# A hybrid layer on one core: the start of the first token block, the stores of its p results, and the last spread of 1/rms

## The chip, the cores and the metric

The kernel runs on one core of a Trainium2 chip. The metric is the time of one execution on the device, in microseconds (us). The engines are named as the profile names them: PE is the matrix engine (PEld its weight loads), DVE the vector engine, ACT the scalar engine, POOL the general engine, SP the engine that only issues transfers. Each engine works through its own queue of instructions in order; a transfer (DMA) is issued by an instruction on SP, ACT or POOL and then runs by itself.

## The reference

One encoder layer over 2048 prompt tokens and, with a state of their own, 64 sample tokens. All is float32, the model width is 1024.

```python
h = rms_norm(x, g_pre)
vA, bA, cA, zA, q, f, iv, zB, gA, gB = split_cols(h @ w_in)          # 10 projections of 1024
yA = (silu(zA) * bA * causal_conv3(cA * vA, conv_w)) @ w_a_out       # path A
S_new, o = hgrn2_scan(S0, silu(q) * scale, 1 - fg, iv, log(fg))      # path B, chunks of 64, 8 heads
   # fg = lb + (1 - lb) * sigmoid(f);  lb from a softmax over lb_raw, the "lower bounds"
yB = (rms(o) * g_onorm * silu(zB)) @ w_b_out
out = (sigmoid(gA) * yA + sigmoid(gB) * yB) @ w_o
x = x + rms_norm(out, g_post)
x = x + (p @ w_ple_proj) * sigmoid(rms_norm(x, g_ple) @ w_ple_gate)  # p: 256 columns per token
```

The outputs are x for both kinds of tokens, the last two rows of the convolution's input and the states S.

## The kernel before

The 2112 tokens are cut into three blocks of 768, 704 and 640. Within a block everything lies with features on the 128 partitions and tokens along the free axis; a block has two token halves (`segs`), and a product covers 128 x 128 weights and one half of 384, 352 or 320 tokens. Each float32 number is split into a rounded high part and a low remainder (`split`: the high part is a copy on ACT, the low part a subtraction on DVE), and each product is three: high x high, high x low, low x high. Many products of the large projections use a Strassen-like scheme of seven products for eight (`sgroup`, `in_turn`).

Tiles come from rings: `rt` gives one of 48 tiles of full block width, `hf` one of 8 of half width, `ps_attn` one of 3 banks for results of products and `ps_gemm` one of 5 others. A Python program writes the instructions; a scheduler orders them per engine by priority and expected readiness. Code under `tc.high_priority()` goes first. `placed()` puts instructions behind the last product so far, `behind_all(marks)` behind the named instructions, and `paced(dma)` makes a transfer wait for the last product so far. `hook()` takes the next entry of a list, so that side work is put between groups of products.

The start (in `hybrid_step`, from line 1417) has these steps:

- ACT issues the loads `vec` (the gain vectors and lb_raw) and `hist_s`. SP issues, in this order, two tiles of p of block 0 (`load_p`, `ph0`), four tiles of `w_ple`, eight tiles of rows of x (`ask_rows`), two of `w_ple`, four of rows, two of `w_ple`, p of block 1, one tile of x by features (`ask_x`), four halves of weights (`ask_w`) and seven tiles of x.
- `split_p` splits p; `held_split(j)` splits tile j of `w_ple`, which is kept for two blocks. The generator `ple` then makes p @ w_ple_proj: each of its eight steps j is 12 products (two halves, two tiles of p, three products each), and its result is copied out of the bank (L1212 on DVE, L1214 on ACT) and stored to memory by POOL (L1219).
- Between the first steps of `first_ple` stand the squares of the rows of x (L1484 on ACT, L1481 and L1482 on DVE), whose mean gives 1/rms; `rstd_of` raises to the power -0.5 on POOL (L682), and `spread` (L693) lays the result over all partitions with products against the identity.
- `first_operands` scales x (L787) and makes its high and low parts and the sums for the seven-product scheme. Meanwhile `plain_group` multiplies the last two column groups of gB as x comes, one feature tile k at a time; before each k `next_k` runs a step of `second_ple` (the same `ple` for block 1) and one step of `first_operands`.
- `constants` makes masks, clears tiles and computes the lower bounds `lb` (L207 to L216).

The end: in the last block `norms` are the final norms of the two token halves and `gate` the last products (w_ple_gate) of each half. `spread_out` gives each hook a number of steps of a norm. In `rms`, one step sums squares over partitions (`col_rstd`, L702) and starts the power on POOL, and the next spreads the result (`spread`, L693, copied by L713). Then eight steps make the operands of the second half's products (L1365 and the split). `final_gate` puts off its merges (L1374, L1375) by a table `held`, from group j to a number of merges; those of the last entry stand behind the copy of the spread, those of earlier ones behind the mean.

Of the kernel before, what the change touches and what calls it, by code (L numbers as in the profile page):

```python
# [18 lines left out]
P = 128  # L19
# [74 lines left out]
def hybrid_step(  # L94
# [73 lines left out]
        return dram.tile([P, BN], F32, tag=f"{kind}{j}", name=nm(kind), bufs=2)[:, : width[0]]  # L168


    ident = const.tile([P, P], F32, tag="ident", name="ident")
    make_identity(nc, ident)
    ones = const.tile([P, 1], F32, tag="ones", name="ones")
# [21 lines left out]
    def constants():  # L195
        for rows, odd, base in ((slice(0, P), 0, 0), (slice(0, CH), 1, -CH), (slice(CH, P), 1, CH)):
            tri = rt(P)
            G.memset(tri, 1.0)
            G.affine_select(
                out=tri, in_=tri, pattern=[[1, P]], compare_op=ALU.is_ge, fill=0.0, base=base, channel_multiplier=-1  # L200
            )
            V.tensor_copy(caus[odd][rows], tri[rows])
        V.memset(keep, 1.0)
        V.memset(keep.rearrange("p (c t) -> p c t", t=CH)[:, :, 0:1], 0.0)
        for t in atts + lone:
            V.memset(t, 0.0)
        V.tensor_tensor(tmp, lb0, lb1, ALU.max)  # L207
        V.tensor_tensor(lb, lb0, tmp, ALU.subtract)
        V.tensor_tensor(omlb, lb1, tmp, ALU.subtract)
        A.activation(lb, lb, AF.Exp)  # L210
        A.activation(omlb, omlb, AF.Exp)
        V.tensor_tensor(tmp, lb, omlb, ALU.add)
        V.reciprocal(tmp, tmp)
        V.tensor_tensor(lb, lb, tmp, ALU.mult)
        V.tensor_scalar(omlb, lb, -1.0, 1.0, ALU.mult, ALU.add)
        V.tensor_scalar(nomlb, lb, 1.0, -1.0, ALU.mult, ALU.add)  # L216
# [269 lines left out]
    def plain_group(i1, i2, hs, sink, raws=None, between=None):  # L486


        w, ps = {}, {}

        def split_of(c, h):
            key = ((i1, i2)[c], h)
            raw = raws[c, h] if raws else load_raw(w_blk[key])
            with nullcontext() if raws else tc.high_priority():
                w[c, h] = split_w(raw, key)

        for c, h in ((0, 0), (1, 0)) if between else ((0, 0), (0, 1), (1, 0), (1, 1)):
            with behind_all(() if between else summed[2] if c else ends[-1]):
                split_of(c, h)

        def add(c, ks):
            for k in ks:
                hi, lo = w[c, k // KH]
                for h in range(2):
                    if (c, h) not in ps:
                        ps[c, h] = ps_gemm()
                    xhi, xlo = hs[k][h]
                    T.matmul(ps[c, h], hi[:, k % KH, :], xhi, start=k == 0, stop=False)
                    T.matmul(ps[c, h], hi[:, k % KH, :], xlo, start=False, stop=False)
                    last[0] = T.matmul(ps[c, h], lo[:, k % KH, :], xhi, start=False, stop=k == KB - 1).ins  # L510

        if between:
            for k in range(KB):
                between()
                for c in range(2):
                    if k == 2:
                        split_of(c, 1)
                    with placed():
                        add(c, (k,))
        for c in range(2):  # L520
            if not between:
                with placed():
                    add(c, range(KB))
            for h in range(2):
                sink(c, h, ps[c, h], None)
# [652 lines left out]
            hooks.extend([None, None, None, piece] * 12)  # L1178


    def load_p(bl, queue):
        raws = [rt(), rt()]
        for k, raw in enumerate(raws):
            queue.dma_start(raw, p_fm[k * P : (k + 1) * P, bl["t0"] : bl["t0"] + bl["n"]])
        return raws

    def ple(bl, ph, kept, held=None, shared=False, spare=()):
# [3 lines left out]
        for j in range(KB):  # L1191
# [23 lines left out]
            if bl["last"]:  # L1215
                kept["p", j] = t
            else:
                kept["p", j] = spill("p", j)
                G.dma_start(kept["p", j], t)  # L1219
                if not shared:  # L1220
                    lows["p", j] = dram.tile([P, 2, P], F32, tag=f"lop{j}", name=nm("low"), bufs=1)
                    SP.dma_start(lows["p", j], lo.bitcast(F32))
# [193 lines left out]

    kepts = [{} for _ in blocks]
    width[0] = blocks[0]["n"]
    A.dma_start(vec, vecs)
    A.dma_start(hist_s, hist0)  # L1420

    with tc.high_priority():
        ph0 = load_p(blocks[0], SP)
        raws = [rt(4 * P).rearrange("p (j k c) -> p j k c", j=2, c=P) for _ in range(KH)]
        raws = [raw[:, j] for raw in raws for j in range(2)]
        rows, xs, w1 = [], [], {}
# [2 lines left out]
        def ask_ple(*js):  # L1429
            for j in js:  # L1430
                SP.dma_start(raws[j], w_ple[j])

        def ask_rows(n):
            for r, c in places[len(rows) : len(rows) + n]:
# [9 lines left out]
            for c in range(2):  # L1444
                w1[c, h] = load_raw(w_blk[GB * 8 + KB - 2 + c, h])

        ask_ple(0, 1, 2, 3)
        ask_rows(8)
        ask_ple(4, 5)
        ask_rows(4)  # L1450
# [2 lines left out]
            ph1 = load_p(blocks[1], SP)  # L1453
        ask_x(1)
        ask_w(0)
        ask_w(1)
        ask_x(7)
        held = []

        def held_split(j):  # L1460
# [6 lines left out]
            out = [(rt(dt=F32R), rt(dt=F32R)) for _ in raws]  # L1467
            return out, [split(raw, *hl) for raw, hl in zip(raws, out)][-1]

        ph, done = split_p(ph0)  # L1470
        with behind_all(done):
            done = [held_split(j) for j in range(2)][-1]
    first_ple = ple(blocks[0], ph, kepts[0], held, True)

    ss = small.tile([P, 2, 6], F32, tag="rows", name="rows", bufs=1)
    for n in range(4):
        with behind_all((*done, *evicted)):
            for i in range(3 * n, 3 * n + 3):
                t, total = rows[i], ss[:, i % 2, i // 2 : i // 2 + 1]
                if i % 3 == 2:  # L1480
                    V.tensor_tensor(t, t, t, ALU.mult)  # L1481
                    V.tensor_reduce(total, t, axis=mybir.AxisListType.X, op=ALU.add)  # L1482
                else:
                    A.activation(t, t, AF.Square, accum_out=total)  # L1484
            if n == 3:
                V.tensor_tensor(ss[:, 0, :], ss[:, 0, :], ss[:, 1, :], ALU.add)
                done = [*done, rstd_of(ss[:, 0, :], ss[:, 0, :], 1.0 / D)]
        with placed():
            run(first_ple, 1)
        with behind_all(done):  # L1490
            for j in (n + 2,) if n < 3 else (5, 6, 7):
                done = held_split(j)
    for _ in range(2):
        with placed():
            run(first_ple, 1)
# [11 lines left out]
    ops = first_operands(hc, rs, xs, hs)  # L1507
    second_ple = sized(blocks[1], ple(blocks[1], ph, kepts[1], held, spare=(1, 3, 5)))

    with behind_all(done):  # L1510
        run(ops, 2)

    def next_k():

        with placed():
            run(second_ple, 2 if len(hs) == 2 else 1)
        if len(hs) < KB:
# [5 lines left out]
        plain_group(GB * 8 + KB - 2, GB * 8 + KB - 1, hs, gate_sink(outs, opened), w1, next_k)  # L1523
    keep_gates(kepts[0], GB, KB - 2, outs)
    run(second_ple)
    with behind_all((*copies, *opened)):
        run(ops)
    constants()
    fills = sized(blocks[0], gates(blocks[0], hc, kepts[0], True))
    for bi, bl in enumerate(blocks):  # L1530
        first, kept = bi == 0, kepts[bi]
# [83 lines left out]
            run(final_gate(bl, segs, xo, h2, kept))  # L1615
        else:

            gate = [final_gate(bl, [s], xo, h2, kept, anew=s is segs[1], held={} if s is segs[1] else {0: 0, 1: 0, 2: 0, 3: 2, 4: 3}) for s in segs]
            spread_out((norms[0], (2, 2, 1, 0, 1, 1, 4, 4)), (norms[1], (0,) * 6 + (1, 1) + (1, 1, 1, 0, 0, 1, 1, 3, 3, 2)))
            run(ple(bl, ph, kept, spare=range(KB)))  # L1620
            run(gate[0], 2)
            with behind_all(copies[:1]):
# [53 lines left out]
```

## Time and profile before

| | us |
|---|---|
| median of three runs (lowest, highest) | 2593.07 (2592.7, 2595.34) |
| the profiled execution | 2591.23 |
| its span, first to last instruction | 2589.5 |
| PE busy in that span | 2567.9 |
| DVE, ACT and POOL busy | 1726.6, 1530.7, 367.5 |

The profile shows one execution on the chip. A page gives sums; views of the trace give the instructions in order of time (start, duration, engine, line, output and inputs, and in brackets the idle time before it and what ended it), the waits (who waited for whom: total, times, longest), groups of instructions by line (count, busy time, mean ns, idle time before them), stretches of time with the busy time of each engine, the granted clock of PE as a share of full speed, and the transfers. `PEq`, `SPq` and the like are the sequencers of the engines, which issue transfers. Durations of products overlap: the step from one start to the next is what counts.

### The profile page before, as it was taken

What the parts mean: (1) busy time and instruction counts of PE and PEld (TensorE: products, weight loads), DVE (VectorE), ACT (ScalarE), POOL (GpSimd) and SP (SyncE); (2) the same over time, 40 slices, a digit from 0 to 9 for tenths busy, and PEclk for the clock granted to TensorE, in tenths of its full rate; (3) what the DMA queues carried; (4) which work ended last, traced back from release to release, by engine and by line L of the source; (5) the groups of instructions that cost most, each with busy time, mean ns of one, the idle gap of its engine ahead of it and who ended that gap; (6) DMA issues with size and microseconds to landing.
All of it is one profiled execution on the core that took longest, in us unless ns stands there. A gap on an engine that the chain in (4) does not pass through costs nothing.

```text
span 2589.5 us, 47473 instructions
## 1 busy us (share of the span) xinstructions
PE 2567.9 (99%) x16414; PEld 2554.4 (99%) x16414; DVE 1726.6 (67%) x3495; ACT 1530.7 (59%) x2973; POOL 367.5 (14%) x675
## 2 busy tenths in 40 slices
PE   8999999999999999999999999999999999999999
PEld 8999999999999999999999999999999999999998
DVE  7788778898767775466464556987345545346967
ACT  6766676454453764466564555576456655446675
POOL 2011111230022021111111221102100000001011
PEclk9999999999999999999999999999999999999999
DMA  8678777898797888877778999989887788999985
GB/s 325 218 262 287 270 255 273 309 375 305 260 347 244 272 313 265 282 251 232 260 225 291 344 388 313 326 290 335 292 270 249 247 271 268 297 299 323 331 267 197
DMA packets 361457, 739.87 MB, mean 286 GB/s; under 512 B 44374, under 2 KB 49024, under 8 KB 361216
## 3 DMA queue, kind: packets, MB, share of 16 engines
q1 hardware_dynamic: 321696, 582.69, 67.5%
q0 software_dynamic: 39232, 154.10, 16.3%
q8 instruction: 129, 2.11, 0.3%
q14 instruction: 112, 0.92, 0.1%
q10 hardware_dynamic: 288, 0.05, 0.0%
HBM read 543.44 MB, written 193.22 MB: 284 GB/s over the span
## 4 chain that ended last, share of the span: by engine, by line
PE 91%; DMA 3%; DVE 3%; issue 2%; ACT 1%; POOL 0%; SPq 0%; DVEq 0%; ACTq 0%; POOLq 0%
PE pg L436 19%; PE pg L438 19%; PE pg L437 19%; PE pg L587 5%; PE pg L586 5%; PE pg L588 5%; PE pg L626 3%; PE pg L624 3%; PE pg L625 3%; PE pa L1129 1%; PE pa L1089 1%; PE pa L1131 1%; PE pa L1075 1%; DMA s<-low 1%; PE pa L1074 1%
## 5 line engine op out<-in xcount | busy, mean ns | idle before, releaser
L436 PE MATMUL pg<-r,hi 128*128 128x320 f32 (+2 forms) x3304 | 1086.0, 329 | 1.5 <-DVE r L484 0.9
L437 PE MATMUL pg<-r,hi 128*128 128x320 f32 (+2 forms) x3304 | 1066.6, 323 | 0.0
L438 PE MATMUL pg<-r,lo 128*128 128x384 f32 (+2 forms) x2356 | 767.8, 326 | 2.6 <-DMA lo<-low 2.6
L267 ACT CAST hi<-raw 128x512 fp32r<-128x512 f32 x730 | 449.7, 620 | 518.8 <-PE pg L437 175.1
L436 PEld LDWEIGHTS pg<-r,hi 128*128 128x128 f32 x3304 | 621.3, 188 | 3.1 <-issue 1.5
L437 PEld LDWEIGHTS pg<-r,hi 128*128 128x128 f32 x3304 | 621.6, 188 | 0.0
L438 PEld LDWEIGHTS pg<-r,lo 128*128 128x128 f32 x2356 | 442.3, 188 | 3.7 <-DMA lo<-low 3.6
L438 PE MATMUL pg<-r,s 128*128 128x352 f32 (+1 forms) x948 | 300.0, 316 | 1.2 <-DMA s<-low 1.1
L587 PE MATMUL pg<-r,hi 128*128 128x320 f32 (+2 forms) x864 | 277.2, 322 | 0.5 <-DVE r L220 0.4
L586 PE MATMUL pg<-r,hi 128*128 128x320 f32 (+2 forms) x864 | 274.9, 322 | 0.0
L220 ACT CAST hi<-raw 128x512 fp32r<-128x512 f32 x252 | 155.5, 620 | 156.0 <-PE pg L625 40.1
L220 DVE TENSOR_TENSOR r<-r,r 128x320 fp32r<-128x320 f32 (+7 forms) x352 | 208.5, 611 | 52.3 <-ACT r L220 51.1
L220 DVE TENSOR_TENSOR lo<-raw,hi 128x512 fp32r<-128x512 f32 x231 | 158.3, 687 | 87.7 <-ACT hi L220 83.9
L220 ACT CAST r<-r 128x320 fp32r<-128x320 f32 (+7 forms) x352 | 185.4, 559 | 50.5 <-DMA r<-w_blk 12.9
L588 PE MATMUL pg<-r,lo 128*128 128x352 f32 (+2 forms) x564 | 180.9, 321 | 1.1 <-DMA lo<-low 1.1
L438 PEld LDWEIGHTS pg<-r,s 128*128 128x128 f32 x948 | 178.1, 188 | 2.1 <-DMA s<-low 2.1
L624 PE MATMUL pg<-r,hi 128*128 128x384 f32 (+2 forms) x512 | 167.3, 328 | 0.2 <-ACT hi L267 0.2
L625 PE MATMUL pg<-r,hi 128*128 128x384 f32 (+2 forms) x512 | 167.3, 327 | 0.0
L220 ACT CAST hi<-s 128x512 fp32r<-128x512 f32 x156 | 96.1, 618 | 120.3 <-PE pg L437 107.0
L587 PEld LDWEIGHTS pg<-r,hi 128*128 128x128 f32 x864 | 162.2, 188 | 2.1 <-DVE r L220 1.6
L586 PEld LDWEIGHTS pg<-r,hi 128*128 128x128 f32 x864 | 161.3, 188 | 1.3 <-ACT r L220 0.9
L450 ACT COPY hf<-pg 128x352 f32<-128x352 f32 (+2 forms) x354 | 157.1, 446 | 1.9 <-PE pg L438 1.6
(398 smaller groups left out, 4113.3 us busy)
## 6 DMA issues: line engine op xcount, KB each, us to landing
raw<-w_blk SPq DMA_DIRECT2D x577, 256.0 KB, 4.1
raw<-S SPq DMA_DIRECT2D x444, 256.0 KB, 4.1
lo<-low SPq DMA_DIRECT2D x422, 256.0 KB, 4.0
s<-low SPq DMA_DIRECT2D x308, 256.0 KB, 4.0
low<-lo SPq DMA_DIRECT2D x271, 256.0 KB, 3.7
S<-s SPq DMA_DIRECT2D x152, 256.0 KB, 3.5
low<-r POOLq DMA_DIRECT2D x54, 256.0 KB, 4.9
r<-w_blk POOLq DMA_DIRECT2D x52, 256.0 KB, 6.8
```

The lines of the kernel that those rows point to most:

```text
L220: return A.copy(hi, src).ins, V.tensor_tensor(lo, src, hi.bitcast(F32), ALU.subtract).ins
L267: A.copy(hi, raw)
L436: add(hi[:, k, :], xhi, start=start and k == 0, stop=False)
L437: add(hi[:, k, :], xlo, start=False, stop=False)
L438: last[0] = add(lo[:, k, :], xhi, start=False, stop=k == KH - 1).ins
L450: copied = A.copy(got[n], ps[bank])
L586: add(hi[:, k, :], xhi, start=start and k == 0, stop=False)
L587: add(hi[:, k, :], xlo, start=False, stop=False)
L588: last[0] = add(lo[:, k, :], xhi, start=False, stop=k == KH - 1).ins
L624: T.matmul(ps, hi[:, k % 4, :], xhi[:, c], start=k == ks[0], stop=False)
L625: T.matmul(ps, hi[:, k % 4, :], xlo[:, c], start=False, stop=False)
L626: last[0] = T.matmul(ps, lo[:, k % 4, :], xhi[:, c], start=False, stop=k == ks[-1]).ins
```

## The change

- Eleven products of a cleared 128 x 128 tile with itself stand first in PE's queue; their result is not read.
- p of block 0 is loaded in four parts, by token halves, with the first tile of `w_ple` behind the first part; the splits follow in the same halves, with the first tile of `w_ple` split after the first part and the second after the fourth. The order of later loads changes too: two tiles of x come between the two pairs of weights.
- The loads `vec` and `hist_s` stand behind these splits, and the lower bounds are a function of their own, placed behind all splits of `w_ple`.
- The results of `ple` for blocks 0 and 1 are not stored at once: `store_parked` stores them from the fourth tile of x on, two or three before each k, each waiting for the last product so far.
- One step of `second_ple` is put ahead of the first operands, and the second half of the first weights is split behind the third tile's operands.
- At the end, the spread of the second half's last 1/rms moves from the hook in group 4 to the hook in group 5, the steps behind it are taken as 4 and 4, and the merges held for it are released after group 5 (four of them) and not after group 4 (three).

```diff
+    idle = hf(P)
+    V.memset(idle, 0.0)
+    unread = ps_attn()
+    for _ in range(11):
+        T.matmul(unread[:, :P], idle, idle, start=True, stop=True)
     ident = const.tile([P, P], F32, tag="ident", name="ident")
...
         for t in atts + lone:
             V.memset(t, 0.0)
+
+    def lower_bounds():
         V.tensor_tensor(tmp, lb0, lb1, ALU.max)
...
                     if k == 2:
-                        split_of(c, 1)
+                        with behind_all(ends[2]):
+                            split_of(c, 1)
...
+    parked = []
+
+    def store_parked(n):
+
+        for _ in range(min(n, len(parked))):
+            paced(G.dma_start(*parked.pop(0)))
...
-                G.dma_start(kept["p", j], t)
+                if held is not None:
+                    parked.append((kept["p", j], t))
+                else:
+                    G.dma_start(kept["p", j], t)
...
-    A.dma_start(vec, vecs)
-    A.dma_start(hist_s, hist0)
 
     with tc.high_priority():
-        ph0 = load_p(blocks[0], SP)
+        ph0 = [rt(), rt()]
...
+        def ask_p(h):
+            for k, raw in enumerate(ph0):
+                SP.dma_start(half(raw, h), p_fm[k * P : (k + 1) * P, h * hn() : (h + 1) * hn()])
+                if k == 0 and h == 0:
+                    ask_ple(0)
...
-        ask_ple(0, 1, 2, 3)
+        assert blocks[0]["t0"] == 0
+        ask_p(0)
+        ask_p(1)
+        ask_ple(1, 2, 3)
         ask_rows(8)
...
         ask_x(1)
         ask_w(0)
+        ask_x(2)
         ask_w(1)
-        ask_x(7)
+        ask_x(5)
...
-        ph, done = split_p(ph0)
+        ph, done = [(rt(dt=F32R), rt(dt=F32R)) for _ in ph0], ()
+        for h in range(2):
+            for k, (raw, (hi, lo)) in enumerate(zip(ph0, ph)):
+                with behind_all(done):
+                    done = split(half(raw, h), half(hi, h), half(lo, h))
+                if k == h:
+                    with behind_all(done):
+                        done = held_split(h)
         with behind_all(done):
-            done = [held_split(j) for j in range(2)][-1]
+            A.dma_start(vec, vecs)
+            A.dma_start(hist_s, hist0)
...
+    split_all = done
...
-    with behind_all(done):
+    with placed():
+        run(second_ple, 1)
+    with behind_all((*done, *copies)):
         run(ops, 2)
 
     def next_k():
 
+        store_parked((0, 0, 0, 2, 2, 3, 3, 3, 3)[len(hs)])
         with placed():
             run(second_ple, 2 if len(hs) == 2 else 1)
...
     run(second_ple)
+    store_parked(len(parked))
     with behind_all((*copies, *opened)):
         run(ops)
     constants()
+    with behind_all(split_all):
+        lower_bounds()
...
-            gate = [final_gate(bl, [s], xo, h2, kept, anew=s is segs[1], held={} if s is segs[1] else {0: 0, 1: 0, 2: 0, 3: 2, 4: 3}) for s in segs]
-            spread_out((norms[0], (2, 2, 1, 0, 1, 1, 4, 4)), (norms[1], (0,) * 6 + (1, 1) + (1, 1, 1, 0, 0, 1, 1, 3, 3, 2)))
+            gate = [final_gate(bl, [s], xo, h2, kept, anew=s is segs[1], held={} if s is segs[1] else {0: 0, 1: 0, 2: 0, 3: 2, 4: 0, 5: 4}) for s in segs]
+            spread_out((norms[0], (2, 2, 1, 0, 1, 1, 4, 4)), (norms[1], (0,) * 6 + (1, 1) + (1, 1, 1, 0, 0, 1, 0, 1, 4, 4)))
```

## The prediction

> **What bounds the kernel now.** I read the page first, then the waits of the matrix engine, the chain of waits over the first 100 us, the order of time there, and the same at the end.
>
> ```profile
> span 2589.5 us, 47473 instructions
> PE 2567.9 (99%) x16414; PEld 2554.4 (99%) x16414; DVE 1726.6 (67%) x3495; ACT 1530.7 (59%) x2973; POOL 367.5 (14%) x675
> ```
>
> PE is busy for all but 21.6 us. So this change can gain only idle time of PE, or time in which PE runs at a lower clock. The waits of PE over the whole run name both places that the diff touches:
>
> ```profile
> PE pa L1207 <- ACT r L220: 6.8, 1, 6.8
> PE pa L693 <- POOL cols L682: 1.1, 2, 0.8
> ```
>
> The first is the start. The chain there, and the rows in order of time:
>
> ```profile
> 0.81 3.45 DMA vec<-vecs
> ...
> 5.46 0.18 DVE lbt L214
> ```
>
> ```profile
> 0.81 0.86 SPq L1184 DMA_DIRECT2D r<-p_fm  x2
> 0.88 0.06 DVE L174 MEMSET ones<- 128x1 f32 x1 [0.88 <-PEq L1664]
> ...
> 2.78 0.45 DVE L206 MEMSET lone<- 128x128 f32 x3
> ...
> 4.90 2.16 ACT L220 CAST r<-r 128x768 fp32r<-128x768 f32 x4
> ...
> 6.80 0.69 PE L1207 MATMUL pa<-r,r 128*128 128x384 f32 x1 [6.80 <-ACT r L220]
> ...
> 8.51 0.52 PE L1207 MATMUL pa<-r,r 128*128 128x384 f32 x1
> ...
> 12.35 0.37 PE L1207 MATMUL pa<-r,r 128*128 128x384 f32 x1
> ...
> 26.54 1.50 PE L693 MATMUL pa<-ident,rows 128*128 128x128 f32 x12
> ```
>
> PE idles 6.80 us: the lower bounds (lbt) stand on the path ahead of the splits of p. Then it steps by 0.32 us a product (12 from 8.51 to 12.35), and by 0.175 after that (the other 81 of the first `ple`'s 96, to 26.54): 5.55 us at half the clock. At 26.54 the spread of 1/rms (L693) begins. At the end of the kernel:
>
> ```profile
> 2537.42 0.31 PE L624 MATMUL pg<-r,hi 128*128 128x320 f32 x1
> ...
> 2541.95 0.31 PE L625 MATMUL pg<-r,hi 128*128 128x320 f32 x1
> 2542.40 0.83 PE L702 MATMUL pa<-ones,r 128*128 128x1 f32 x6
> ...
> 2543.47 0.31 PE L625 MATMUL pg<-r,hi 128*128 128x320 f32 x1
> 2544.62 1.24 PE L693 MATMUL pa<-ident,cols 128*128 128x128 f32 x6 [0.84 <-POOL cols L682]
> ```
>
> ```profile
> 2545.05:2548.45 3.40, 3.40 (x16) 3.40 (x15) 2.55 (x7) 0.62 (x1) 1.59 (x4) 0.51 0.33 118
> 2541.62:2545.03 3.41, 2.43 (x17) 1.90 (x16) 2.38 (x7) 1.10 (x3) 1.15 (x2) 1.00 0.99 368
> ...
> 2516.90:2525.00 8.10, 7.87 (x57) 7.55 (x58) 3.54 (x9) 5.06 (x13) 4.27 (x7) 1.00 0.75 237
> ```
>
> The columns of the last fence are the stretch, its length, the busy times of PE, weight loads, DVE, ACT and POOL, the clock, the DMA share and GB/s. PE steps every 0.146 us (31 from 2537.42 to 2541.95), so it could go on at about 2543.62 and goes on at 2544.62: 1.0 us lost to the power of -1/2 on POOL. A stretch of 3.41 us with PE busy 2.43 us is followed by 3.40 us at a granted clock of 0.51. That is 3.40 x 0.49 = 1.67 us more.
>
> **Weighed against the skill.** The Trainium skill, "TensorE: Matmul & The Clock Gate", Part 1, says the gate watches free-running windows of 3413 ns, releases the clock after one busy window and halves it after one idle window. The width agrees with the 3.40 us row; the condition does not, since the window ahead of it was 2.43 us busy. By the page's rule of a whole idle window the end could gain only the 1.0 us, and the sum below would be smaller by 1.67 us. I go by the row.
>
> **The change, part by part.**
>
> *Products of zeros.* They wait for one memset. DVE's first row is at 0.88 and a 128x128 memset is 0.45 / 3 = 0.15 us, so PE starts at about 1.1. Eleven products in f32 are 22 instructions (three columns of L693 give six). The L693 row at half clock is 1.24 us for six, 0.207 each: 4.55 us, to 5.65. They add that to PE in a stretch where it was idle to 6.80, so they cost nothing unless the real operands are there before 5.65; that loss is at most about 1 us.
>
> *Clock.* Before, the clock rose 5.55 us after the first product. From 1.1 that gives 6.65; counted in windows of 3.4 us with unknown phase it is 4.5 to 7.9. At worst PE makes real products at half speed from 5.65 to 7.9, 1.1 us lost.
>
> *p by halves, lower bounds behind the splits, small loads behind them.* The first product needs half of one p tile, one w_ple tile and their splits, not two whole p tiles and nine small lbt operations. Four loads take the place of two on SP, and at about 0.43 us an issue (0.86 for two) the loads queued behind them, rows of x first, are asked for up to 0.9 us later; but they no longer share the queue with `vecs`. I count these as equal. The first split can then start near 3.5 to 4, and PE starts real work at 5.65, set by the products of zeros.
>
> *What is late next.* 96 products x 0.174 = 16.7 us from 5.65 would end at 22.35: the lower bound. Before, cold PE hid ACT; now ACT sets the pace. It carries squares, splits of w_ple and copies in order:
>
> ```profile
> L1484 ACT ACTIVATE r<-r 128x512 f32<-128x512 f32 x8 | 5.0, 628 | 1.7 <-DMA r<-x_tok 1.7
> L220 ACT CAST r<-r 128x256 fp32r<-128x256 f32 x6 | 2.4, 409 | 0.2 <-DMA r<-w_ple 0.2
> L1214 ACT COPY r<-pa 128x384 f32<-128x384 f32 x4 | 1.9, 476 | 1.1 <-PE pa L1209 0.9
> ```
>
> ```profile
> 1.73 1.28 ACT L210 ACT_TABLE_LOAD   x1 [1.73 <-PEq L1664]
> 8.42 0.63 ACT L1484 ACTIVATE r<-r 128x512 f32<-128x512 f32 x1 [1.36 <-DMA r<-x_tok]
> 18.56 0.41 ACT L220 CAST r<-r 128x256 fp32r<-128x256 f32 x1 [0.16 <-DMA r<-w_ple]
> ```
>
> From 8.42 to 18.97 are 10.55 us, about 9.0 of them work (idle: 1.7 less the 1.36 ahead of 8.42, 0.2 and 1.1). The table load may now stand in front of the first square and the two issues of small loads (0.9 us, as two on SP) after the splits, which end near 6.0: 6.0 + 0.9 + 1.28 = 8.2, about as early as the row of x came before. Then 8.2 + 9.0 = 17.2 for the last split of w_ple, the sixth some 0.7 earlier, and with its DVE half and waits PE starts the sixth of eight steps at about 17.3 and ends at 17.3 + 3 x 2.09 = 23.6. The upper end is 26.54, no gain. I take 23.6, nearest to ACT's own row: **2.9 us gained** (bounds 0 and 4.2).
>
> *Stores of p behind the loads of x.* POOL's sixteen stores leave this stretch:
>
> ```profile
> p<-r POOLq DMA_DIRECT2D x8, 384.0 KB, 6.5
> p<-r POOLq DMA_DIRECT2D x8, 352.0 KB, 5.1
> r<-x_fm SPq DMA_DIRECT2D x8, 384.0 KB, 13.1
> ```
>
> ```profile
> 15.00:40.00 25.00, 25.00 (x151) 24.70 (x151) 18.40 (x33) 17.50 (x42) 6.86 (x11) 1.00 1.03 408
> ```
>
> The DMA engines are full from 15 to 40 us (share 1.03). The stores are 8 x 384 and 8 x 352 KB = 6.0 MB, 14.8 us at 408 GB/s. Without this an earlier PE would meet x_fm (13.1 us to land), so the move keeps the 2.9 us rather than adding to them. The stores wait on PE's progress on POOL's queue; nothing urgent stands behind them there until the masks. Tiles are held longer, in a ring of 48; I count about as many allocations between as there is room and take 0, with at most the rival's price below. One more step of `ple` for block 1 ahead of the first operands moves PE work only: 0. `lower_bounds` later is nine short DVE operations of 0.2 us on an engine with gaps: 0, at most 1.6 us where there are none. The second half of `w1` split later: 0 for the same reason.
>
> *Last spread later.* The spread goes one product group later, 24 x 0.146 = 3.5 us, so POOL is done and PE no longer waits: 1.0 + 1.67 = 2.7 us. But what feeds on it starts later against a PE that is earlier:
>
> ```profile
> 2545.90 0.49 DVE L713 COPY r<-pa 128x320 f32<-128x320 f32 x1 [0.86 <-PE pa L693]
> ...
> 2562.26 0.48 DVE L220 TENSOR_TENSOR r<-r,r 128x320 fp32r<-128x320 f32 x1
> ```
>
> ```profile
> L1365 DVE SCALAR_TENSOR_TENSOR r<-r,vec,r 128x320 f32<-128x320 f32 x8 | 4.4, 545 | 0.0
> L220 DVE TENSOR_TENSOR lo<-raw,hi 128x512 fp32r<-128x512 f32 x6 | 4.0, 687 | 0.4 <-ACT hi L220 0.4
> L220 DVE TENSOR_TENSOR r<-r,r 128x320 fp32r<-128x320 f32 x8 | 3.9, 486 | 1.1 <-ACT r L220 1.1
> L1374 DVE TENSOR_TENSOR r<-r,r 128x320 f32<-128x320 f32 x6 | 2.8, 484 | 0.0
> ```
>
> DVE needed 16.84 us from the copy to the last operand, 1.5 idle. PE wanted that operand at about 2563.1: from 2545.86 some 109 products were ahead of it (the rest of a group, two groups of 24, seven eighths of a double one), ten at 0.27 and the rest at 0.146. After: the group ends near 2546.4, the spread 0.6 later, the copy at 2547.05; with the same order the last operand comes at 2563.9, with no idle time 2562.4, and with two weight splits and one merge (2.0 us) put behind it 2560.4. PE now wants it at 2563.1 - 2.7 = 2560.4. So the new wait is 0 to 3.5 us; I take 1.3, nearer to the lower end because those operations aren't needed by then and ACT's weight casts come earlier. **Net 1.4 us gained** (bounds: 2.7 gained, and 2.5 lost where 3.5 us of waiting halves the clock once more, 2.7 - 3.5 - 1.67).
>
> **Sum.** 2.9 + 1.4 = 4.3 us. The profiled execution is 2591.23 us (span 2589.5 and 1.73 around it) and becomes 2586.9; it is 1.84 us under the median of the three runs, so against 2593.07 I say 2588.8.
>
> **Rivals.**
>
> *Both gains whole* (4.2 and 2.7): ACT's order lets the copies through and DVE puts merges behind. 2593.07 - 6.9 = 2586.2. For it: DVE's 1.5 us idle. Against: the 9.0 us of ACT.
>
> *The start gives nearly nothing.* The zero products do not raise the clock, or PE's waits for w_ple lower it once more, as 2.43 of 3.41 us did at the end. Then 1.67 us of the 2.9 are lost and the end gives 0: 1.2 us, 2591.9. For it: that row. No row shows products of zeros.
>
> *The half clock at the end stays.* It would not come from the 1.0 us of waiting but from the thin products of L702 (one column, 0.83 us for six), which remain, or from the phase of the stretch. Then 1.67 us are missing from the forecast: 2590.5. For it: PE was already idle 0.3 us ahead of L702, and that stays. Against: the stretch from 2516.90, which begins with the same six products and has a shorter wait, keeps a clock of 1.00. The page's rule above also has no place for a drop after a wait of 1.0 us.
>
> *Slower: the parked stores hold up the next weights.*
>
> ```profile
> raw<-w_blk SPq DMA_DIRECT2D x1, 256.0 KB, 6.1
> ```
>
> ```profile
> 60.43 0.33 PE L508 MATMUL pg<-r,hi 128*128 128x384 f32 x1
> ```
>
> That load, of 43.0, lands at 49.1 and is used at 60.43 after a cast and a subtraction of 1.3: 10.0 us of room. If all 14.8 us of stores went ahead of it, PE would wait 4.8 us, with 1.67 at half clock 6.5, less 4.3: 2593.07 + 2.2 = 2595.3. It decides from 10 us of delay on. Against it: the stores are spread over six steps of 4 us.
>
> **How the numbers follow.** Forecast 0.44, both whole 0.28, nearly nothing at the start 0.14, half clock stays 0.08, slower 0.06. About 0.2% (5.2 us) is what a measurement of this kernel can tell from no change, so under 2587.9 is faster: all of "both whole" and a fifth of the forecast's spread (2586.5 to 2591), 0.37; slower by that much only if the stores and DVE both miss, 0.04; the same 0.59. The range runs from 2585.3 to 2593.0, the ends of the cases less the slower one.
>
> **What would show it.** Right: zero products from 1.1 to about 5.7, first real product there, steps of 0.17 us by 8, L693 near 23.6; x_fm landing in much less than 13 us; no wait of PE for POOL at the end and no stretch at 0.51. Wrong: PE waiting for ACT in the first `ple` beyond 2 us, for raw near 58, for DVE L220 in the last group by k, or a clock under 1 there.

## The result: 14 us slower

The changed kernel takes 2607.06 us (median of 6 runs, 2605.32 to 2609.67), the kernel before 2592.89 us beside it (6 runs, 2591.69 to 2595.34): a ratio of 1.0055, 95% interval 1.0042 to 1.0067. Forecast were 2588.8 us, in a range of 2585.3 to 2593.0. Line numbers have moved: the products of `ple` are now L1223 to L1225, their copies by ACT L1230, the squares of the rows of x L1519, the spread of 1/rms L702, and the loads of `vec` and `hist_s` L1506 and L1507.

The page of the changed kernel, the span and the busy times. The span is 18.5 us above that of the profile before, more than the 14.2 us between the medians: the execution profiled here is the slowest of its six, 2.6 us over their median, and the one before lies 1.7 us under its own.

```profile
span 2608.0 us, 47525 instructions
PE 2573.0 (99%) x16436; PEld 2556.3 (98%) x16436; DVE 1726.5 (66%) x3498; ACT 1531.5 (59%) x2975; POOL 366.0 (14%) x675
```

PE is now idle for 35.0 us of its span instead of 21.6. Its waits name one of them (total, times, longest):

```profile
PE pa L1223 <- ACT r L1230: 17.4, 3, 14.4
```

In order of time, PE and then ACT:

```profile
1.13 4.40 PE L176 MATMUL pa<-hf 128*128 128x128 f32 x22 [1.13 <-DVE hf L173]
5.29 0.42 PE L1223 MATMUL pa<-r,r 128*128 128x384 f32 x1
...
29.23 0.69 PE L1223 MATMUL pa<-r,r 128*128 128x384 f32 x1 [14.42 <-ACT r L1230]
...
35.16 0.45 PE L1223 MATMUL pa<-r,r 128*128 128x384 f32 x1
...
43.66 1.50 PE L702 MATMUL pa<-ident,rows 128*128 128x128 f32 x12
```

```profile
9.85 0.63 ACT L1519 ACTIVATE r<-r 128x512 f32<-128x512 f32 x1 [1.98 <-DMA r<-x_tok]
...
13.31 0.19 ACT L1519 ACTIVATION_READ_ACCUMULATOR r<-r 128x1 f32 x1
28.28 0.38 ACTq L1506 DMA_DIRECT2D vec<-vecs  x1
28.70 0.48 ACT L1230 COPY r<-pa 128x384 f32<-128x384 f32 x1 [15.21 <-DMA r<-x_fm]
```

ACT does nothing from 13.50 to 28.28. Its next instruction is no computation: it issues the load of `vec`, and only behind that comes the copy that frees a PSUM tile for PE. The bracket names what released ACT, a load of x_fm, which has nothing to do with `vec`. The chain of waits says the same:

```profile
16.21 5.48 DMA r<-x_fm
21.70 6.55 DMA r<-x_fm
28.28 0.38 ACTq L1506
28.70 0.49 ACT r L1230
29.23 0.69 PE pa L1223
```

The link is in the built program, not in the data: the loads that SP and ACT issue take turns on eight semaphores, and a load is issued only when the one before it on its semaphore has landed. The change put `vec` behind the splits of p; the scheduler placed it behind four squares. By then SP had asked for many loads, and the turn of `vec` fell on the semaphore of an x_fm tile that was itself issued at 21.70, when the tile of 16.21 had landed, and that landed 6.55 us later.

Then the clock. PE was idle from 14.8, and the clock fell (columns: stretch, length, busy PE, PEld, DVE, ACT, POOL, clock, DMA share, GB/s):

```profile
15.00:20.00 5.00, 0.00 (x0) 0.00 (x0) 0.33 (x1) 0.00 (x0) 0.00 (x0) 0.83 1.05 391
20.00:25.00 5.00, 0.00 (x0) 0.00 (x0) 0.00 (x0) 0.00 (x0) 0.00 (x0) 0.50 1.04 396
...
30.00:35.00 5.00, 5.00 (x17) 5.00 (x17) 3.80 (x7) 4.60 (x15) 0.00 (x0) 0.50 0.58 197
```

From 29.23 to 35.16 are 18 products at 0.32 us or more instead of 0.175: 5.93 - 18 x 0.175 = 2.8 us. So 14.4 + 2.8 = 17.2 us; the first `ple` ends, and the spread begins, at 43.66 instead of 26.54, which is 17.1 us later. The end is 1.4 us shorter (below), and the rest of the difference of the spans is 2.8 us in between; 1.3 of them are a wait of PE for a copy at 71.47 (in the line of waits above, it is part of what the sum of 17.4 has beside the 14.4), the others are of a size that comes and goes from profile to profile.

### The profile page after: what moved, and what is told of

It reads as the page before. It is cut to its first block, busy times and chain, and to the rows that moved or that the text cites. A ratio compares the mean times of both kernels' runs of the same rounds, so it can differ in the third digit from the quotient of the medians.

```text
span 2608.0 us, 47525 instructions
## 1 busy us (share of the span) xinstructions
PE 2573.0 (99%) x16436; PEld 2556.3 (98%) x16436; DVE 1726.5 (66%) x3498; ACT 1531.5 (59%) x2975; POOL 366.0 (14%) x675
## 4 chain that ended last, share of the span: by engine, by line
PE 87%; DMA 5%; DVE 4%; issue 2%; ACT 1%; SPq 0%; POOL 0%; DVEq 0%; ACTq 0%; POOLq 0%
PE pg L444 18%; PE pg L446 18%; PE pg L445 18%; PE pg L596 4%; PE pg L595 4%; PE pg L597 4%; PE pg L634 3%; PE pg L635 3%; PE pg L633 3%; DMA lo<-low 1%; PE pa L1098 1%; PE pa L1138 1%; PE pa L1140 1%; PE pa L1084 1%; DMA low<-lo 1%
```

## The experiments

Theory A: the 14 us are the wait of ACT's issue of `vec`, and nothing else in the change costs microseconds. Its rivals were that some other part does (p by halves, parked stores, the end). Theory B came after the first four runs: the start gains nothing for a second reason. All ratios are against the kernel before on the same chip.

| run | time, us | ratio (95%) | first `ple` done, us |
|---|---|---|---|
| 1 e1_vec_first | 2592.81 | 1.0003 (0.9994 to 1.0011) | 26.72 |
| 2 e2_vec_late_alone | 2611.37 | 1.0073 (1.0058 to 1.0089) | 46.58 |
| 3 e3_vec_on_pool | 2594.06 | 1.0007 (0.9997 to 1.0017) | 26.42 |
| 4 e4_end_alone | 2592.09 | 1.0000 (0.9992 to 1.0009) | 26.89 |
| 5 e5_weights_ahead_of_rows | 2591.32 | 1.0003 (0.9993 to 1.0013) | 27.17 |
| 6 e6_no_zero_products | 2593.93 | 1.0007 (0.9998 to 1.0015) | 27.09 |
| 7 e7_stores_at_once | 2589.85 | 0.9995 (0.9984 to 1.0005) | 27.75 |
| 8 e8_no_early_step | 2592.93 | 1.0002 (0.9993 to 1.0012) | 26.31 |
| 9 e9_squares_last | 2589.79 | 0.9992 (0.9983 to 1.0001) | 24.77 |
| 10 e10_squares_last_no_zeros | 2591.45 | 0.9995 (0.9986 to 1.0004) | 26.69 |
| 11 e11_squares_between | 2590.24 | 0.9989 (0.9979 to 1.0000) | 23.11 |
| e11_again | 2588.48 | 0.9989 (0.9980 to 0.9998) | 23.19 |
| e4_end_alone_again | 2591.81 | 0.9995 (0.9986 to 1.0004) | 26.03 |
| before_again | 2592.08 | one run | 26.87 |

The last column is the start of the spread of 1/rms, the row that the prediction read at 26.54 in the kernel before. Four profiles have before's start (26.54, 26.89, 26.03, 26.87): less than 0.9 us of difference there tells nothing. In runs 9 and 10 the start holds a wait of 1.6 us for 1/rms, shown below.

### 1 to 3: where `vec` and `hist_s` are issued

Run 1 is the changed kernel with the two loads back at the front of ACT's order; run 2 is the kernel before with only these loads moved; run 3 is the changed kernel with the loads left in place but issued by POOL, whose loads use other semaphores.

```diff
 # 1: the changed kernel
+    A.dma_start(vec, vecs)
+    A.dma_start(hist_s, hist0)
     with tc.high_priority():
...
-        with behind_all(done):
-            A.dma_start(vec, vecs)
-            A.dma_start(hist_s, hist0)
 # 2: the kernel before
-    A.dma_start(vec, vecs)
-    A.dma_start(hist_s, hist0)
...
             done = [held_split(j) for j in range(2)][-1]
+        with behind_all(done):
+            A.dma_start(vec, vecs)
+            A.dma_start(hist_s, hist0)
 # 3: the changed kernel
-            A.dma_start(vec, vecs)
-            A.dma_start(hist_s, hist0)
+            G.dma_start(vec, vecs)
+            G.dma_start(hist_s, hist0)
```

> The changed kernel, with the two small loads (vec, hist_s) issued by ACT at its very start, as before the change; all else as changed. Theory: in the changed kernel ACT stood 14.4 us at the issue of vec, because the semaphore lane that this load got was held by a load of x; PE then waited 14.4 us and made 18 products at half clock (2.7 us). So 17.1 us come back: about 2590 us, 0.1% under the kernel before, no wait of PE over 2 us after its first product, L693 near 26.5 - 1.5 = 25. Rival: rows of x landed 1.4 us later in the changed kernel (9.83 against 8.40) and ACT is the bound of the first stretch, so that most of the time would have been lost anyway: not more than 10 us back, 2597 or over.

> The kernel before, with one thing changed: vec and hist_s are issued by ACT behind the first two splits of w_ple. Theory: the same wait arises without anything else of the change: in ACT's order vec stands behind the first two squares of rows, and its lane is that of the third late load of x, so ACT stands from about 9 us until that load lands (25 to 29 us): 15 to 20 us slower, 2608 to 2613. Rival: the stall in the changed kernel needs the other parts (four loads of p, parked stores), or the delay comes from late landing of vec itself; then under 3 us slower.

> The changed kernel, with vec and hist_s issued by POOL in place of ACT, at the same place of the program. Theory: POOL's transfers have lanes of their own, so neither ACT nor POOL waits, and SP's loads keep all their lanes: as fast as with the loads at ACT's start or up to 1 us faster, 2588.5 to 2590. Rival (the place behind the splits is what costs): as slow as the changed kernel, 2607.

Runs 1 and 3 give the 14 us back; run 2 makes 19 us out of the old kernel, with no other edit. In run 2 ACT stands at the same place, in order of time, and so does PE in its waits:

```profile
25.53 0.38 ACTq L1472 DMA_DIRECT2D vec<-vecs  x1
...
26.88 0.48 ACT L1214 COPY r<-pa 128x384 f32<-128x384 f32 x1 [17.53 <-DMA r<-x_fm]
...
30.82 0.21 ACT L210 ACTIVATE lbt<-lbt 128x8 f32<-128x8 f32 x1 [1.93 <-DVE lbt L208]
```

```profile
PE pa L1207 <- ACT r L1214: 17.6, 2, 15.9
```

Of the 17.6 us, 15.9 are the wait behind the issue. The other 1.7 are the rival of run 2 in small: `vec` itself lands late, at 30.40, and in the old kernel the lower bounds, which need it, still stand in ACT's order ahead of the next copy (the last row). The changed kernel has its lower bounds behind all splits and no such wait.

Theory A holds. But without the wait the change ends where it began: run 1 takes 2592.81 us, no less than before, where about 2590 were expected.

### 4: the end alone

Only the two lines of `gate` and `spread_out` at the end of the diff, in the kernel before.

> The kernel before, with only the end changed (spread one group later, merges held to group 5). Theory, from the two traces laid side by side: 2.6 us won at the spread (no wait for POOL, no stretch at half clock) and 1.15 us lost again where PE now waits for DVE: 1.3 us faster, 2591.5. Rival: the stretch at half clock is chance and most executions do not have it; then 0 to 0.5 us, 2592.5 or more.

Timed twice, it is the same as before: 1.0000 and 0.9995. In the trace the end is shorter. The last column sums of the run (L702 in the kernel before and in run 4, L711 in the changed one), from each to the end of its span:

```profile
2544.99 0.83 PE L702 MATMUL pa<-ones,r 128*128 128x1 f32 x6 [0.16 <-DVE r L724]
2548.99 0.83 PE L693 MATMUL pa<-ident,cols 128*128 128x128 f32 x6
```

```profile
2562.25 0.83 PE L711 MATMUL pa<-ones,r 128*128 128x1 f32 x6
...
2566.25 0.83 PE L702 MATMUL pa<-ident,cols 128*128 128x128 f32 x6
```

Run 4: 2590.7 - 2544.99 = 45.71 us; changed: 2608.0 - 2562.25 = 45.75; before: 2589.5 - 2542.40 = 47.10. That is 1.4 us, the prediction's net term. It is not chance: in the three profiles with the old end (before, before_again, run 2) the time from these column sums to the end is 47.10, 47.18 and 47.16 us, and the clock falls to 0.51, 0.51 and 0.56 behind the spread; in the thirteen with the new end it is 45.5 to 45.8 us and the clock stays at 1.00. So the rival of run 4 is refuted. The second profile of the kernel before shows what the first did (the column sums, then the clock behind the spread):

```profile
2543.22 0.83 PE L702 MATMUL pa<-ones,r 128*128 128x1 f32 x6 [0.54 <-DVE r L724]
```

```profile
2545.80:2549.20 3.40, 3.40 (x16) 3.40 (x15) 2.38 (x7) 0.62 (x1) 1.43 (x3) 0.51 0.35 127
```

In the new end the spread waits for nothing, and in the changed kernel the stretches at and behind it stay at full clock, where before had 0.51; a little later PE misses the operands that the prediction named:

```profile
2562.25:2565.65 3.40, 3.40 (x24) 3.40 (x25) 1.76 (x5) 1.09 (x3) 1.92 (x3) 1.00 0.89 330
2565.65:2569.05 3.40, 3.40 (x27) 3.40 (x26) 1.93 (x5) 1.23 (x3) 0.28 (x1) 1.00 0.81 229
...
2575.85:2579.25 3.40, 3.06 (x19) 2.27 (x17) 3.40 (x9) 2.69 (x6) 0.00 (x0) 1.00 0.33 98
```

```profile
2576.45 0.42 PE L634 MATMUL pg<-r,hi 128*128 128x320 f32 x1 [0.16 <-DVE r L228]
...
2579.21 0.42 PE L635 MATMUL pg<-r,lo 128*128 128x320 f32 x1 [0.16 <-DVE lo L228]
```

In that last stretch DVE is busy throughout. The 19 of the row counts the products that run in it; PE starts 16, where 3.40 / 0.146 = 23 would fit, which is 7 x 0.146 = 1.0 us lost.

The times do not show these 1.4 us, and do not refute them: they would be a ratio of 0.9995, which lies in both intervals, as 1 does. What hides so small a gain is seen in the second profile of run 4 (span 2597.0 us, 7.5 us above before's). At 915 us PE waits for DVE, and its clock halves (the wait, then the stretches):

```profile
915.01 2.13 PE L702 MATMUL pa<-ones,r 128*128 128x1 f32 x12 [1.45 <-DVE r L724]
```

```profile
911.00:914.41 3.41, 2.56 (x16) 2.27 (x15) 2.93 (x4) 3.41 (x7) 0.00 (x0) 1.00 0.73 189
914.41:917.82 3.41, 2.81 (x15) 2.81 (x16) 2.68 (x7) 3.38 (x7) 1.24 (x2) 0.69 0.58 209
917.82:921.23 3.41, 3.41 (x15) 3.41 (x14) 0.00 (x0) 0.38 (x1) 2.31 (x4) 0.50 0.69 237
921.23:924.64 3.41, 3.41 (x21) 3.41 (x21) 1.19 (x2) 1.58 (x3) 0.00 (x0) 0.81 0.52 167
```

Over the last three stretches that is 3.41 x (0.31 + 0.50 + 0.19) = 3.4 us more. The first profile of the same kernel has no such spell there, and the 11 or 12 times of one kernel spread over 5 to 12 us. A gain of 1.4 us needs more runs than the 23 here.

### 5 to 8: why the start gains nothing

Run 5 asks for all w_ple tiles ahead of the rows of x and places each step's squares behind its product; runs 6, 7 and 8 each undo one part of the change. All four stand on run 1.

```diff
 # 5
-        ask_ple(1, 2, 3)
-        ask_rows(8)
-        ask_ple(4, 5)
-        ask_rows(4)
-        ask_ple(6, 7)
+        ask_ple(1, 2, 3, 4, 5, 6, 7)
+        ask_rows(12)
...
 # 6
...
-    for _ in range(11):
-        T.matmul(unread[:, :P], idle, idle, start=True, stop=True)
 # 7
-                if held is not None:
+                if False:
                     parked.append((kept["p", j], t))
                 else:
                     G.dma_start(kept["p", j], t)
 # 8
-    with placed():
-        run(second_ple, 1)
-    with behind_all((*done, *copies)):
+    with behind_all(done):
         run(ops, 2)
```

> The kernel of the first experiment (vec and hist_s at the very start of ACT's order), with all eight w_ple tiles asked for ahead of the twelve rows of x, and with each step's three squares placed behind the step's product and split instead of ahead of them. Theory B (the start gains nothing because TensorE, now ready and at full clock at 5 us, waits for rows of x and w_ple tiles that the order of the loads brings too late: ACT stands 1.80 us for a row at 9.36 us, the last w_ple tile lands at 18.6 us): the first ple then runs without those waits and ends about 4 us sooner than before's, near 22.5 us; if nothing behind it is bound by loads, the time is about 2588.5 to 2589.5. Rival C (what follows, the products of x, is bound by the landing of x_fm and w_blk, whatever the first ple does): the ple ends sooner, but the lead is gone by 60 us and the time stays within 1 us of the first experiment's 2592.8.

> The kernel of the first experiment without the 22 products of zeros. By theory B (loads bound the start) the half clock of the first products only fills time that TensorE else waits for ACT and the loads: the 18th product comes some 2 us later, but the first ple ends within 0.7 us of the first experiment's end (26.7 us) and the time within 1 us of its 2592.8. By the prediction's own reckoning (the clock is the bound): about 2.5 us later, 2595.

> The kernel of the first experiment with the first block's eight p results stored as soon as each is made, as in the kernel before, instead of behind the loads of x. If the parking was worth something, the loads of x_fm and w_blk land up to 4 us later here (1.6 MB of stores beside loads at about 390 GB/s) and the time rises by 1 to 4 us. If it was worth nothing, as the first experiment's missing gain says, the time stays within 1 us of 2592.8.

> The kernel of the first experiment without the step of the second ple that the change pulled ahead of the first products of x. The prediction put this step at nothing. In the first experiment's trace TensorE's lag against before grows by about 1.2 us between 30 and 54 us, in the stretch of the products of x, where one step of the ple fewer stands between. If the pulled step does that, the lag at 54 us is 1.2 us smaller and the time is about 2591.5; if the lag comes from elsewhere (DVE's sums), nothing changes.

No time differs from before's by what can be told, so the traces must speak. Run 6: without the zeros the first `ple` ends at 27.09 instead of 26.72, which is within the spread. The clock that the zeros raise is worth nearly nothing here, as theory B said. Run 1 shows what is worth more, ACT and PE in order of time:

```profile
9.36 0.63 ACT L1518 ACTIVATE r<-r 128x512 f32<-128x512 f32 x1 [1.80 <-DMA r<-x_tok]
```

```profile
11.13 0.44 PE L1223 MATMUL pa<-r,r 128*128 128x384 f32 x1 [1.57 <-ACT r L1230]
...
13.18 0.42 PE L1223 MATMUL pa<-r,r 128*128 128x384 f32 x1 [0.74 <-ACT r L1518]
...
18.26 0.42 PE L1223 MATMUL pa<-r,r 128*128 128x384 f32 x1 [0.45 <-DVE r L1228]
```

Copies of the `ple` results stand in ACT's order behind squares, and the squares wait for rows of x that have not landed. In the kernel before, whose first products go at half pace, PE has no wait over 0.2 us from its first product to the spread; here it does. Run 5 shows that the new order of the loads, with each step's squares behind its product, doesn't mend it: with the weights there in time the rows come later still, ACT stands 2.75 us for the first, and the `ple` ends at 27.17.

```profile
11.39 0.63 ACT L1520 ACTIVATE r<-r 128x512 f32<-128x512 f32 x1 [2.75 <-DMA r<-x_tok]
```

Run 7: with the stores at once the loads of x_fm land late again (a median of 12.4 us after their issue, for 7.6 with parking and 13.1 before), and the `ple` ends 1.0 us later, barely more than the spread; the time, 2589.85, went the other way. What the parking is worth stays open. The first row is of run 1, the second of run 7:

```profile
r<-x_fm SPq DMA_DIRECT2D x8, 384.0 KB, 7.6
```

```profile
r<-x_fm SPq DMA_DIRECT2D x8, 384.0 KB, 12.4
```

Run 8: the step pulled ahead costs run 1 this wait, which run 8's trace does not have; in time it isn't seen.

```profile
54.54 0.43 PE L1223 MATMUL pa<-r,r 128*128 128x352 f32 x1 [1.31 <-ACT r L1230]
```

### 9 to 11: the squares behind the copies

Run 9 is run 5 with the squares three steps further back and without the early step; run 10 is run 9 without zeros; run 11 has the squares one step earlier than run 9.

```diff
 # 11 (in 9: from n = 3 on, up to n == 6)
-    for n in range(4):
-        with behind_all((*done, *evicted)):
-            for i in range(3 * n, 3 * n + 3):
+    for n in range(7):
+        with placed():
+            run(first_ple, 1)
+        with behind_all(done):
+            for j in (n + 2,) if n < 3 else (5, 6, 7) if n == 3 else ():
+                done = held_split(j)
+        with behind_all((*done, *copies, *evicted)):
+            for i in range(3 * (n - 2), 3 * (n - 2) + 3) if 2 <= n < 6 else ():
...
```

> The order of loads of the fifth experiment (all w_ple tiles ahead of the rows), the squares moved three steps further back (behind the steps 3 to 6 of the first ple instead of 0 to 3, so that no copy of a product stands behind a row that has not landed), and no early step of the second ple. Theory B': what held the start in all versions is that the copies of the ple results stand in ACT's and DVE's order behind squares of rows that land at 11 to 19 us. Without that the first ple runs at full pace from 5.5 us, 8 steps of 2.1 us, and ends near 22.5 us, 4 us sooner than before's 26.5; with the end's 1.4 us the time is 2586.5 to 2587.5. Rival C: the last rows land at 19.3 us, their squares, the spread and the products of x come after them as before, and x_fm lands to 32 us: TensorE waits there instead, the lead at 60 us is under 1 us and the time is about 2590.5 to 2592.

> The kernel of the ninth experiment without the 22 products of zeros. Where nothing else holds the start, the clock does: some 18 products at half pace (0.32 us for 0.175 us) cost 2.5 us, so the first ple ends 2 to 2.7 us later than in the ninth. By rival C (loads and rows hold it) it ends at the same time within 0.7 us.

> The ninth experiment with the squares one step earlier (behind the steps 2 to 5 of the first ple) and the split of the second block's p one step later. In the ninth TensorE stood 1.59 us for the 1/rms (POOL rows at the spread, 24.77 us), because the last squares ended at 22.6 us on ACT. If that wait was the step's only price, it is gone here, and the lead at 60 us grows from the ninth's 1.3 us to about 3 us; with the end's 1.4 us the time is 2587 to 2588.5. Rival C (the landing of x_fm or of the second block's p takes its place): the lead at 60 us stays within 0.5 us of the ninth's and the time at about 2590.

Run 9's PE has no wait in the first `ple` beyond 0.32 us, but then one for 1/rms, and the spread begins at 24.77 where 22.5 was expected; run 10 has the same wait 1.9 us later (its lines are 5 lower). So in the trace the zeros are worth 1.9 us (2 to 2.7 were expected) once no copy waits behind a row, and nothing that can be told while one does; the times of runs 9 and 10 do not differ. Run 9, run 10, run 11:

```profile
24.77 0.94 PE L702 MATMUL pa<-ident,rows 128*128 128x128 f32 x6 [1.59 <-POOL rows L691]
```

```profile
26.69 0.94 PE L697 MATMUL pa<-ident,rows 128*128 128x128 f32 x6 [1.59 <-POOL rows L686]
```

```profile
23.11 1.50 PE L702 MATMUL pa<-ident,rows 128*128 128x128 f32 x12
```

In run 11 the trace lists no wait of PE from the first zero to 60 us, and the spread begins 3.4 us sooner than before. It was timed twice, and a second profile was taken of the kernel before.

> The eleventh kernel once more. If a mechanism of the middle takes the lead back, the lag against before at 950 us and at 1800 us is again about -2.5 us and 0 us, and the time again 1 to 2 us under before's. If it was chance, the lead of 3.5 us at 100 us is still 2 us or more at 2500 us in this profile, and the time is 3 to 5 us under before's in the mean over both.

> The fourth kernel (before with only the end changed) once more. If the end's 1.4 us is real, the time is 0.5 to 2 us under before's in the mean over both times; if something ahead of it takes it back, it is within 0.5 us of it, and the lag against before ahead of the end is again 1 to 2 us.

> The kernel before once more, for a second profile of it. If the lag of some microseconds that comes and goes in the middle of the other profiles is no effect of an edit, the two profiles of this kernel differ there as much; the stretch at about half clock at the spread of the last 1/rms (2566 to 2569 us) should come again, and the end, from the 350th last product, should again take 58.5 us.

Both times of run 11 give 0.9989; the second one's interval ends under 1 (0.9980 to 0.9998). The median of its 22 runs is 2589.2 us, that of the 36 runs of before beside them 2591.7. So, as far as two timings tell, it is faster than the kernel before, by 2.5 us, which is half of the 3.4 + 1.4 us that the trace shows at the two places. In both profiles some of that lead is lost on the way, at one place in the same manner. Near 940 us fifteen of the sixteen profiles wait for a weight's low part, the kernel before (first row) as run 11's second profile:

```profile
941.09 0.42 PE L438 MATMUL pg<-r,lo 128*128 128x352 f32 x1 [1.92 <-DMA lo<-low]
```

```profile
936.89 0.43 PE L446 MATMUL pg<-r,lo 128*128 128x352 f32 x1 [2.25 <-DMA lo<-low]
```

The 4 us behind it, in before, in run 11 and in its second profile:

```profile
942.00:946.00 4.00, 4.00 (x26) 4.00 (x26) 3.68 (x6) 2.80 (x5) 0.99 (x2) 1.00 1.03 374
```

```profile
938.00:942.00 4.00, 4.00 (x17) 4.00 (x16) 2.93 (x5) 2.41 (x5) 1.08 (x2) 0.57 1.02 377
```

```profile
938.00:942.00 4.00, 4.00 (x17) 4.00 (x17) 2.62 (x4) 2.09 (x4) 0.80 (x2) 0.60 1.03 389
```

The same kind of wait leaves the clock at 1.00 in before and halves it for a while in both profiles of run 11, which is 4 x 0.4 = 1.6 us. The edit does not decide that. The two profiles of run 4 are of one kernel; the first keeps its clock behind this wait, the second does not:

```profile
942.00 0.43 PE L438 MATMUL pg<-r,lo 128*128 128x352 f32 x1 [1.58 <-DMA lo<-low]
```

```profile
942.00:946.00 4.00, 4.00 (x25) 4.00 (x26) 3.68 (x6) 3.46 (x8) 1.63 (x3) 1.00 1.05 397
```

```profile
948.43 0.43 PE L438 MATMUL pg<-r,lo 128*128 128x352 f32 x1 [1.83 <-DMA lo<-low]
```

```profile
948.43:952.43 4.00, 4.00 (x17) 4.00 (x18) 3.68 (x6) 3.12 (x7) 1.63 (x3) 0.67 1.05 403
```

Of the fifteen profiles with the wait, eight keep the clock at 1.00 and seven drop to about 0.5. Neither the length of the wait nor its moment in the span decides: run 7 keeps 1.00 behind 2.26 us that end at 942.83, run 10 drops behind 1.82 us that end at 942.45. What does decide is not shown. The kernel before, profiled again, shifts by -1.2 to +1.5 us against its first profile along the way and ends 0.8 us later, so shifts of that size are no effect of an edit. Against that first profile run 11 still leads by 2.3 us (2.7 in its second profile) at 950 us, and by 0.0 us (1.3) at 1800 us; its second profile was expected either to repeat the first or to keep the lead whole, and does neither.

## Why the prediction was wrong

- **The step that failed** is the cost of the moved small loads: "the two issues of small loads (0.9 us, as two on SP) after the splits". I priced an issue by its duration and set nothing for what it waits for, though an issue stands in its engine's order like any other instruction and ACT's order holds the copies that PE needs. Measured: 14.4 us of PE's wait and 2.8 us of half clock. The sign of being wrong was named, PE waiting for ACT in the first `ple` beyond 2 us, but none of the rivals had the cause; the slower one put its price on the parked stores, which cost nothing that shows.
- **The start's 2.9 us** failed a second time, on its own. "Four loads take the place of two ... I count these as equal", and the first square was set at 8.2 us. Without the wait for `vec` it came at 9.36, and ACT's idle time was no longer at the front but between the copies. Measured: 26.72 in run 1 for 26.54 before, no gain. The rival that the start gives nearly nothing has this number, but not its reason: the zeros did raise the clock. That 2.9 us and more were there to be had is right: run 11 has 3.4 us.
- **Products of zeros.** Predicted from 1.1 to 5.65, measured 1.13 to 5.53 with the speed-up in it; the first real products already step by 0.17 us. (The clock is read from these steps: the profile's column shows 1.00 here from the start, in the kernel before too, where the steps are 0.32 us.) The zeros also hold the first real product back, at 5.01 in run 1 for 4.37 in run 6, within the 1 us that was allowed. The pace and the clock were right; "ACT sets the pace" was right too, but its price was not.
- **Stores of p.** x_fm lands in 6.6 us for 13.1 (the row `r<-x_fm` of the transfers), as predicted. Worth 1.0 us at the end of the first `ple` in run 7's trace, and not shown in time.
- **The early step of `second_ple`**, counted at 0, costs one wait of 1.3 us in the trace.
- **The end's 1.4 us net** was right in the trace: 47.10 - 45.75 = 1.35 us. The wait for POOL and the stretch at 0.51 (1.0 + 1.67 us) are gone, and DVE took about 1.3 us back where it was expected, 7 products' time (1.0 us) of it in the one stretch shown. That the 1.3 us was met so closely is partly luck, since its bounds were 0 and 3.5. The rival that the half clock would stay is refuted by the stretches at 1.00 in all thirteen profiles with the new end. In the times these 1.4 us are not shown.
- **The rule for the half clock.** The Trainium skill, "TensorE: Matmul & The Clock Gate", Part 1, lets the clock fall after an idle window. The 14.4 us agree with it; the spell at 915 us, behind a stretch busy for 2.56 of 3.41 us, does not, like the row of before that the prediction went by.

## What to carry to other kernels

Before you move a load to a compute engine's order, ask what its issue can wait for, semaphores that are reused in turn included, and what stands behind it there; a load that nobody needs soon is cheapest at the very front, or on an engine that nobody waits for. A faster engine shows waits that a slow one covered: price the cover, by asking which instructions of its feeders stand behind data that lands late. And where a gain is a few us against a spread of ten, read it at its place in the trace, and say that the time does not show it.

## What was not expected of the hardware

How much a short wait of PE can cost, and that it need not: behind 1.45 us at 915 us the clock stood at 0.69, 0.50 and 0.81 for three stretches of 3.41 us, 3.4 us lost, and behind 2.25 us at 937 us 1.6 us were lost; behind the same kind of wait eight of fifteen profiles lost nothing more, one of them behind 2.26 us. At the end of the old kernel, by contrast, the drop came in all three profiles. So two executions of one kernel differ by more than the gains that were looked for here, while one place can be the same each time.
